# Row-centred squares: stores issued from ScalarE's queue in pairs of rows

## The chip, the cores and the metric

The kernel runs on one core of a Trainium2 chip. The metric is device time in microseconds (us) of that core. The kernel before takes 82.98 us, the median of three runs that lie between 82.96 and 83.04 us. A separate profiled execution took 83.14 us; its span, from the first to the last recorded instruction, is 81.4 us. All times of single instructions below are counted from the start of that span.

## What is computed

```python
def reference(x, axis):                       # x: 1024 x 4096, float32; axis = -1
    mean = np.mean(x, axis=axis, keepdims=True)
    return ((x - mean) ** 2).astype(np.float32)
```

Every row of 4096 numbers is averaged, the average is subtracted from the row, and the differences are squared. The input is 16.78 MB and so is the output; every byte is read once from HBM (the chip's memory) and written once.

## The kernel before

The 1024 rows are split into two tiles. A tile has 128 partitions, and each partition holds four whole rows (`Q = 4`), 4 x 4096 numbers or 64 KB. Both tiles have a buffer of their own, so that both loads can be asked for at the start, and the squares are written over the input in the same buffer.

```python
x_t = x.rearrange("(p n q) d -> n p (q d)", p=P, q=Q)
out_t = out.rearrange("(p n q) d -> n p (q d)", p=P, q=Q)

for i in range(ntiles):                       # ntiles = 2
    x_tile = io.tile([P, Q * D], F32)
    if i == 0:
        nc.sync.dma_start(out=x_tile[:, :HEAD], in_=x_t[i][:, :HEAD])       # HEAD = 512 numbers
        nc.sync.dma_start(out=x_tile[:, HEAD:], in_=x_t[i][:, HEAD:])
    else:
        end = Q * D - HEAD
        nc.scalar.dma_start(out=x_tile[:, end:], in_=x_t[i][:, end:])
        nc.sync.dma_start(out=x_tile[:, :end], in_=x_t[i][:, :end])
    # ... (tiles.append)
```

A load is thus one large transfer of 62 KB for each partition, issued from SP's queue, and a small one of 2 KB for each partition. The small one of the second tile is issued from ScalarE's queue. Then each row (128 rows at a time, one in each partition) takes two steps: VectorE (DVE in the profile) adds it up and yields minus the mean; ScalarE (ACT) squares the row with that as its bias. Of the fourth row of a tile, VectorE does the last eighth.

```python
for i in range(ntiles):
    for q in range(Q):
        row = tiles[i][:, q * D:(q + 1) * D]
        # ... (pairs, neg_mean: scratch and one number for each partition)
        inorder(nc.vector.tensor_tensor_reduce(out=pairs, in0=row[:, :HALF], in1=row[:, HALF:],
                scale=-inv_d, ..., accum_out=neg_mean))                    # L66
        cut = D if q < Q - 1 else LAST
        nc.scalar.activation(out=row[:, :cut], in_=row[:, :cut], func=ACT.Square,
                bias=neg_mean, scale=1.0)                                  # L77
        if cut < D:
            rest = row[:, cut:]
            nc.vector.tensor_scalar_add(out=rest, in0=rest, scalar1=neg_mean)   # L86
            nc.vector.tensor_mul(out=rest, in0=rest, in1=rest)                  # L87
    nc.sync.dma_start(out=out_t[i], in_=tiles[i])                          # L88: one store a tile
```

A framework places the semaphore waits and orders each engine's instructions; it may move an instruction among its neighbours on the same engine.

Of the kernel before, what the change touches and what calls it, by code (L numbers as in the profile page):

```python
# [2 lines left out]

os.environ.setdefault("NEURON_RT_ULTRASERVER_MODE", "4")

# [4 lines left out]

F32 = mybir.dt.float32
ACT = mybir.ActivationFunctionType
ADD = mybir.AluOpType.add


@with_exitstack
def kernel(
    ctx: ExitStack,
    tc: tile.TileContext,
    x: bass.AP,  # L20
    axis: bass.AP,
    out: bass.AP,
):

    nc = tc.nc

    B, D = x.shape
    P = nc.NUM_PARTITIONS
    Q = 4
    HEAD = 512
    HALF = D // 2
    LAST = D - D // 8
    assert B % (P * Q) == 0
    ntiles = B // (P * Q)
    inv_d = 1.0 / float(D)

    x_t = x.rearrange("(p n q) d -> n p (q d)", p=P, q=Q)
    out_t = out.rearrange("(p n q) d -> n p (q d)", p=P, q=Q)

    io = ctx.enter_context(tc.tile_pool(name="io", bufs=ntiles))
    scratch = ctx.enter_context(tc.tile_pool(name="scratch", bufs=1))
    stats = ctx.enter_context(tc.tile_pool(name="stats", bufs=ntiles * Q))

    tiles = []
# [3 lines that stand above are left out]
            nc.sync.dma_start(out=x_tile[:, :HEAD], in_=x_t[i][:, :HEAD])  # L52
# [5 lines that stand above are left out]
        tiles.append(x_tile)  # L58

    inorder = tc.keep_in_program_order  # L60
# [3 lines that stand above are left out]
            pairs = scratch.tile([P, HALF], F32)  # L64
            neg_mean = stats.tile([P, 1], F32)
            inorder(nc.vector.tensor_tensor_reduce(  # L66
                out=pairs,
                in0=row[:, :HALF],
                in1=row[:, HALF:],
                scale=-inv_d,  # L70
                scalar=0.0,
                op0=ADD,
                op1=ADD,
                accum_out=neg_mean,
            ))
            cut = D if q < Q - 1 else LAST
            nc.scalar.activation(  # L77
                out=row[:, :cut],
                in_=row[:, :cut],
                func=ACT.Square,  # L80
                bias=neg_mean,
                scale=1.0,
            )
            if cut < D:
                rest = row[:, cut:]
                nc.vector.tensor_scalar_add(out=rest, in0=rest, scalar1=neg_mean)  # L86
                nc.vector.tensor_mul(out=rest, in0=rest, in1=rest)  # L87
        nc.sync.dma_start(out=out_t[i], in_=tiles[i])  # L88


# [1 line left out]
_INS = ['x', 'axis']  # L92
_OUTS = [((1024, 4096), 'float32')]

_NUMBERS = {'axis': -1}


# [26 lines left out]
```

## Time and profile before

| | before |
|---|---|
| device time, median of 3 | 82.98 us |
| profiled span | 81.4 us |
| VectorE busy | 20.8 us (26%) |
| ScalarE busy | 29.4 us (36%) |
| DMA queue of SP (q1) | 33.29 MB |
| DMA queue of ScalarE (q10) | 0.26 MB |
| HBM read / written | 16.78 MB / 16.78 MB |
| bytes per time over the span | 412 GB/s |

How to read it: a core has 16 DMA engines, and both queues feed them. The profile names the two queues by number: q1 is SP's and q10 is ScalarE's. A "packet" of the DMA records is one piece that a DMA engine moves at once; here it is the part of a transfer that belongs to one partition, so a transfer over 128 partitions is 8 packets on each of the 16 engines, and a last record of 4 bytes on each engine counts the semaphore that tells of completion. An issuing instruction (L53, L57, L88) only hands over a transfer: it is short, and the transfer lands later.

### The profile page before, as it was taken

Reading aid. Unit: us, or ns where it says so; the run is one execution under the profiler, and the core shown is the slowest. Engines: PE = TensorE matmul, PEld = TensorE weight load, DVE = VectorE, ACT = ScalarE, POOL = GpSimd, SP = SyncE. Lnnn points to the kernel's source line nnn. Section 1 sums busy time; section 2 is a strip of 40 time slices with the busy share of each in tenths; the row PEclk is TensorE's granted clock in tenths of the full one; section 3 lists DMA queues with packets and bytes.
Section 4 is the critical chain, followed back from the end, with each engine's and each line's share of the span. In section 5 each row is a group of like instructions: output and inputs, shape, how many; then the busy total and the mean of one; then the engine's idle time right before and its main releaser. Section 6 shows DMA issues by size and latency. Waiting matters only on the chain.

```text
span 81.4 us, 87 instructions
## 1 busy us (share of the span) xinstructions
DVE 20.8 (26%) x20; ACT 29.4 (36%) x9; POOL 0.2 (0%) x4
## 2 busy tenths in 40 slices
DVE  0000000000059999600039999700000000000000
ACT  0000000000054999999502999999600000000000
POOL 0000000000000000000000000000000000000000
DMA  1974999999759999995799993899996599999390
GB/s 22 704 343 187 499 499 499 499 499 437 343 218 499 499 499 499 499 406 250 343 516 515 515 515 161 354 515 515 515 516 290 258 483 515 515 515 419 161 451 0
DMA packets 864, 33.55 MB, mean 412 GB/s; under 512 B 96, under 2 KB 96, under 8 KB 352
## 3 DMA queue, kind: packets, MB, share of 16 engines
q1 hardware_dynamic: 720, 33.29, 95.0%
q10 hardware_dynamic: 144, 0.26, 1.1%
HBM read 16.78 MB, written 16.78 MB: 412 GB/s over the span
## 4 chain that ended last, share of the span: by engine, by line
DMA 49%; ACT 13%; ACTq 4%; DVE 3%; SPq 1%; issue 0%
DMA x_tile<-in_x_dram 49%; ACT x_tile L77 13%; ACTq L119 4%; DVE pairs L66 3%; SPq L53 1%; SPq L52 0%; DVE neg_mean L66 0%
## 5 line engine op out<-in xcount | busy, mean ns | idle before, releaser
L77 ACT ACTIVATE x_tile<-x_tile,neg_mean 128x4096 f32<-128x4096 f32 (+1 forms) x8 | 28.2, 3590 | 5.7 <-DVE neg_mean L66 5.7
L66 DVE CUSTOM_DVE_ANT_0 pairs<-x_tile 128x2048 f32<-128x2048 f32 x8 | 18.3, 2292 | 31.6 <-DMA x_tile<-in_x_dram 31.4
L77 ACT ACT_TABLE_LOAD x1 | 1.3, 1283 | 23.2 <-DMA x_tile<-in_x_dram 23.2
L87 DVE TENSOR_TENSOR x_tile<-x_tile 128x512 f32<-128x512 f32 x2 | 1.4, 692 | 0.1
L86 DVE TENSOR_SCALAR x_tile<-x_tile,neg_mean 128x512 f32<-128x512 f32 x2 | 1.0, 488 | 0.1
L66 DVE DVE_READ_ACCUMULATOR2_ANT neg_mean<- 128x1 f32 x8 | 0.7, 82 | 0.0
L105 POOL MEMSET const-bfloat16-1.0<- 128x1 bf16 x1 | 0.1, 102 | 0.0
L105 POOL MEMSET const-uint8-127<- 128x1 uint8 x1 | 0.1, 102 | 0.0
L105 POOL MEMSET const-float32-0.0<- 128x1 f32 x1 | 0.1, 99 | 0.2 <-issue 0.2
L105 POOL MEMSET const-float32-1.0<- 128x1 f32 x1 | 0.1, 99 | 0.0
## 6 DMA issues: line engine op xcount, KB each, us to landing
x_tile<-in_x_dram SPq DMA_DIRECT2D x2, 7936.0 KB, 31.1
x_tile<-in_x_dram ACTq DMA_DIRECT2D x1, 256.0 KB, 3.8
x_tile<-in_x_dram SPq DMA_DIRECT2D x1, 256.0 KB, 3.6
out_dram<-x_tile SPq DMA_DIRECT2D x2, 21.9
```

What stands on the lines that cost most here:

```text
L53: nc.sync.dma_start(out=x_tile[:, HEAD:], in_=x_t[i][:, HEAD:])
L66: inorder(nc.vector.tensor_tensor_reduce(out=pairs, in0=row[:, :HALF], in1=row[:, HALF:], scale=-inv_d, scalar=0.0, op0=ADD, op1=ADD, accu ...
L77: nc.scalar.activation(out=row[:, :cut], in_=row[:, :cut], func=ACT.Square, bias=neg_mean, scale=1.0,)
L86: nc.vector.tensor_scalar_add(out=rest, in0=rest, scalar1=neg_mean)
L87: nc.vector.tensor_mul(out=rest, in0=rest, in1=rest)
L105: nc = _bacc.Bacc("TRN2", target_bir_lowering=False, num_devices=1)
L119: with _tile.TileContext(nc) as tc:
```

## The change

The store of a whole tile from SP's queue at the end of the tile is removed. In its place, after every second row, two rows (32 KB for each partition) are stored from ScalarE's queue. Two stores of 8.39 MB become four of 4.19 MB; the bytes are the same. The aim is that squared rows leave while the second tile is still being loaded, and that SP's queue holds loads alone, so that a store need not stand behind a load.

```diff
             if cut < D:
                 rest = row[:, cut:]
                 nc.vector.tensor_scalar_add(out=rest, in0=rest, scalar1=neg_mean)
                 nc.vector.tensor_mul(out=rest, in0=rest, in1=rest)
-        nc.sync.dma_start(out=out_t[i], in_=tiles[i])
+            if q % 2 == 1:
+                part = slice((q - 1) * D, (q + 1) * D)
+                nc.scalar.dma_start(out=out_t[i][:, part], in_=tiles[i][:, part])
```

In the built program, ScalarE's instructions then stand in this order (the rows of the first tile are r0 to r3, those of the second s0 to s3; the stores are A, B, C and D):

```
square r0, r1, r2
store A (r0, r1)      waits for the squares of r0 and r1
square r3
wait for the second tile's large load
square s0             waits for VectorE's mean of s0
store B (r2, r3)      waits for the square of r3
square s1, s2
store C (s0, s1)      waits for the squares of s0 and s1
square s3
store D (s2, s3)      waits for VectorE's part of s3 and for the square of s3
```

## The prediction, made before the changed kernel had run

> **What bounds the kernel now.** I read the engine totals first, then the chain of waits, then the queue's own waits, and last the busy times by stretch, because the first three name a suspect and only the last shows whether it is full.
>
> The page's totals show no compute engine near its limit:
>
> ```profile
> DVE 20.8 (26%) x20; ACT 29.4 (36%) x9; POOL 0.2 (0%) x4
> q1 hardware_dynamic: 720, 33.29, 95.0%
> q10 hardware_dynamic: 144, 0.26, 1.1%
> DMA 49%; ACT 13%; ACTq 4%; DVE 3%; SPq 1%; issue 0%
> ```
>
> The first line is busy time; the next two are the DMA queues with packets, MB and share of 16 engines' span, 96.1% together; the last is the chain that ended last. Its shares add up to only about 71%, or 58 us: the chain stops at the issue of the last store, at 58.4 us. What follows stands in the queue's own waits:
>
> ```profile
> SPq L88 <- DVE x_tile L87: 41.8, 2, 29.4
> SPq L119 <- DMA out_dram<-x_tile: 21.7, 2, 19.3
> SPq L88 <- ACT x_tile L77: 11.7, 2, 5.8
> ```
>
> The middle line is the end of the kernel waiting for the last store to land. The third line looks like a chance: SP waits for ScalarE before it may issue a store. But whether an earlier issue would help depends on whether the DMA engines are idle meanwhile. So I asked for stretches: from the first load's regular packets to its end, the whole second load, the first store, and all from the first packet to the last.
>
> ```profile
> core 0: us, DVE busy (x) ACT busy (x) POOL busy (x), PEclk, DMA share, GB/s
> 4.08:22.79 18.71, 0.00 (x0) 0.00 (x0) 0.00 (x0) 1.00 1.00 434
> 22.79:41.50 18.71, 10.38 (x10) 15.36 (x5) 0.00 (x0) 1.00 1.00 433
> 40.93:60.25 19.32, 10.38 (x10) 14.08 (x4) 0.00 (x0) 1.00 1.01 434
> 1.74:80.25 78.51, 20.76 (x20) 29.44 (x9) 0.00 (x0) 1.00 1.00 427
> 80.25:81.40 1.15, 0.00 (x0) 0.00 (x0) 0.00 (x0) 1.00 0.00 0
> ```
>
> The last two columns before the line's end are the share of the 16 DMA engines that is busy, and GB/s. They are full, share 1.00, from 1.74 to 80.25 us, through loads and stores alike. Where the first store follows the second load, at 40.93 to 41.50 us, no engine has a gap: SP had issued that store at 39.73 us, before the load was out. The dips in the page's 40 slices, down to 161 GB/s, are only the beat of long packets: a packet is counted in the slice where it starts, and a 62 KB packet takes 2.34 us. **The bound is the sum of bytes through 16 full DMA engines**, with 1.74 us ahead and 1.15 us after.
>
> **What the Trainium skill says.** "DMA: Bandwidth & Descriptors", section "Issuing engines are not separate DMA queues": transfers issued by different engines run on the same 16 DMA engines, and a second issuing engine saves only issue time. The trace agrees as far as it goes: an issue lasts 0.35 to 0.42 us, in the shade of a transfer. The same page, "Where 436 GB/s comes from", puts the ceiling at 435.2 GB/s; the trace has 434 for loads and for stores. The same page, "Queues, rings and completion order": each engine takes packets from its queues in turn. The trace agrees at the start, where 2 KB packets of q1 and q10 alternate on an engine, one by one and 84 ns long mostly, so with no visible cost of changing queues; there both were loads. "Perfetto Trace Analysis", section "DMA Instruction — HWDGE (DVE, Sync)": a DMA engine here doesn't wait on semaphores, the issuing sequencer does. So waits on ScalarE's queue hold back the stores behind them. No run so far shows that for a store on ScalarE's queue.
>
> **The change, part by part.** (1) *Packet cost.* Per packet the trace has 84 ns for 2,048 bytes, 2,342 ns for 63,488 and 2,418 ns for 65,536. A straight line through the first two has 36.75 ps a byte and 8.7 ns fixed, and gives 2,417 ns for the third, so it holds. A new store packet of 32,768 bytes then takes 1,213 ns, two of them 2,426 against 2,418. Each engine has 16 store packets now and 32 after: 16 more at 8.7 ns is 0.14 us; two more completion records of 9 ns make it 0.16 us. No byte is saved.
>
> (2) *Store A.* ScalarE squares r0 and r1 from 25.63 us; two squares take 7.31 us (the chain's own piece for the second tile), so the issue is at 32.9 us instead of 39.73. The first load took 1.0 us from its issue at 0.73 to its first packet at 1.75, so A's packets come at about 34.0. The second load's packets start at 22.2 us and every 2.34 us after; the sixth of eight starts at 33.9, so about three of A's packets get between the load's last three. The load lands 3 x 1.21 = 3.6 us later, at 45.1 instead of 41.5, and the squares of the second tile start at 44.25 + 3.64 = 47.9. This loses nothing by itself: DMA engines do other bytes in that time.
>
> (3) *Store B.* It is ready when r3 is squared, 39.7 us, but stands behind ScalarE's wait for the second load and behind the square of s0. It is issued between 45.6 us (load landed, plus the 0.42 us that VectorE took to start) and 47.9 us, with packets 1.0 us later, 48.9 at worst. At 45.1 us five of A's packets are left, 5 x 1.21 = 6.1 us, enough until 51.2 us (50.6 on the earliest engines). So B is there 1.7 us before the engines would run dry.
>
> (4) *Stores C and D.* Squares of s0 and s1 end at 47.9 + 7.3 = 55.2 us, and C is wanted when B's eight packets are through, 51.2 + 9.7 = 60.9. All squares end at 47.9 + 14.1 = 62.0, and D is wanted at 70.6. Both have slack, so ScalarE's four issues (0.35 us each) and the 3.6 us later start are off the path. D's packets then end at 80.3 to 80.4 us, against 80.25 before.
>
> *Sum.* 82.98 + 0.16 for packets + about 0.1 for changes of direction, below: 83.2 us. The intended gain has no place to come from, because the first store never waited behind idle DMA engines.
>
> **The rivals.** *A. Engines run dry before B.* Turn-taking by packet is seen for equal packets only. If instead the two queues share by bytes, the load's last 7.5 us become 15.0, it lands at 49.0, A has 2.2 us left, and B's packets come at up to 49.4 + 2.3 (one row sum of 2.29) + 1.0 = 52.7, which is 1.5 us late: 84.7 us. If stores had the right of way, the load would land at 51.2 and B come at 54.9: 3.7 us, or 86.9. The order of instructions speaks for this rival, the alternating packets at the start against it; and if ScalarE's sequencer goes past the square of s0 to issue B while that square waits, 2.3 us of it vanish.
>
> *B. Loads and stores together are faster than either alone.* They go in opposite directions, and 434 GB/s was seen with one direction at a time. If reads and writes didn't share a limit, the load's 7.5 us would be hidden beside A: as low as 75 to 76 us. Against it: loads and stores run at the same 27.1 GB/s for an engine, as one limit inside the engine would make it, and at the crossing at 41 us nothing went faster.
>
> *C. Mixing directions costs.* At that crossing 11 of the 16 first store packets took 2,453 to 2,465 ns instead of 2,418, 40 ns more. With some six changes of direction on an engine this is up to 0.24 us; I took 0.1 of it. If every packet of the stretch is slowed by several per cent, it is half a microsecond.
>
> *D. ScalarE becomes the bound.* It would need D's issue later than 70 us; 8.6 us of slack speak against it.
>
> **Range and chances.** The low end, 82.8, allows the 0.16 us to be hidden and some noise; the high end, 84.7, is B late by sharing in bytes. Within 2% is 81.3 to 84.6, which holds my account with and without rival C. Slower by over 2% needs most of rival A: 0.10. Faster by over 2% needs rival B: 0.04. The rest is 0.86.
>
> **What would show it.** In the changed profile: DMA share still 1.00 in every stretch from 1.7 to 80 us, at 434 GB/s; q10 with about 17 MB; store packets of 1.21 us; the second load landing near 45 us and the first row sum of the second tile starting near 45.6; B issued between 45.6 and 47.9; the last landing near 80.4 and a span of 81.6. A share below 1 near 50 us is rival A, and shows how late B came; over 450 GB/s between 34 and 45 us is rival B; packets above 1.25 us there are rival C. I'd be wrong above all if packets of unlike size aren't taken in turn, or if opposite directions don't share the engine's limit.

## The result, and the profile after

The changed kernel takes 84.92 us, median of six runs (84.81 to 85.32), beside 82.98 us for the kernel before (82.93 to 83.04). The ratio is 1.0245, with a 95% interval of 1.0219 to 1.0271: slower by 1.94 us. The prediction was 83.2 us with a range of 82.8 to 84.7, and 0.86 for "within 2%"; the measured time lies above the range.

The page of the changed kernel, the same parts as before (busy time, queues, chain):

```profile
DVE 20.8 (25%) x20; ACT 29.4 (35%) x9; POOL 0.2 (0%) x4
q1 hardware_dynamic: 432, 16.52, 48.6%
q10 hardware_dynamic: 720, 17.04, 47.7%
DMA 55%; DVE 10%; issue 6%; ACT 4%; SPq 1%; ACTq 0%
```

The compute engines do the same work in the same time, and the stores' 16.78 MB have moved from q1 to q10, as they should. The chain now has 55% of waiting for loads where it had 49%. The timeline of the changed kernel around the second tile (start, duration, engine, line, instruction, and in brackets what ended the idle time before it) shows what became of the load and of store B:

```profile
32.87 0.34 ACTq L90 DMA_DIRECT2D out_dram<-x_tile  x1
...
47.16 2.29 DVE L66 CUSTOM_DVE_ANT_0 pairs<-x_tile 128x2048 f32<-128x2048 f32 x1 [13.42 <-DMA x_tile<-in_x_dram]
...
49.50 3.71 ACT L77 ACTIVATE x_tile<-x_tile,neg_mean 128x4096 f32<-128x4096 f32 x1 [9.89 <-DVE neg_mean L66]
49.50 0.34 ACTq L90 DMA_DIRECT2D out_dram<-x_tile  x1
...
56.83 0.34 ACTq L90 DMA_DIRECT2D out_dram<-x_tile  x1
...
63.60 0.34 ACTq L90 DMA_DIRECT2D out_dram<-x_tile  x1
```

Store A is issued at 32.87 us, as computed. The second tile's first row sum starts at 47.16 us, not 45.6. Store B is issued at 49.50, in the very instant in which the square of s0 starts: it did stand behind that square's wait. The obvious suspicion, that the DMA engines ran dry before B, is answered by the stretches of the changed kernel (columns as in the prediction; a packet is counted where it starts):

```profile
33.70:41.56 7.86, 0.04 (x1) 5.91 (x2) 0.00 (x0) 1.00 0.98 325
42.80:81.00 38.20, 10.37 (x10) 14.08 (x4) 0.00 (x0) 1.00 1.00 434
```

The second stretch, which has B's start in it, is full at 434 GB/s. In the first one the engines are as full, share 0.98, but move 325 GB/s. **Busy and slow together: the packets themselves took longer.** The packet records say which. From 5 us to the end of the stores no engine is idle for more than 0.01 us. The 16 load packets that began at 33.8 to 34.5 us took 2.82 to 3.80 us instead of 2.34, the next 16 took 2.54 to 3.81; the last 16, from 41.56 us on, took 2.34 again, although they took turns with store packets, and every store packet took 1.213 us. All load packets together lasted 31.3 us longer than in the kernel before, which is 1.96 us on each of the 16 engines; 1.83 of it lies in the first 32 of those packets, the rest in excesses of under 0.2 us elsewhere.

That accounts for the loss. Load packets +1.96 and store packets +0.03 make 1.99 us for an engine. The last store packet ended at 81.89 us instead of 80.23, 1.66 later, and the large load packets of this profile began 0.34 us earlier than in that of before (3.13 instead of 3.47). What remained was why load packets were stretched, once, when the stores joined.

### The profile page after: what moved, and what is told of

The parts are those of the page before. It is cut to its first block, busy times and chain, and to the rows that moved or that the text cites. A ratio compares the mean times of both kernels' runs of the same rounds, so it can differ in the third digit from the quotient of the medians.

```text
span 83.0 us, 88 instructions
## 1 busy us (share of the span) xinstructions
DVE 20.8 (25%) x20; ACT 29.4 (35%) x9; POOL 0.2 (0%) x4
## 3 DMA queue, kind: packets, MB, share of 16 engines
HBM read 16.78 MB, written 16.78 MB: 404 GB/s over the span
## 4 chain that ended last, share of the span: by engine, by line
DMA 55%; DVE 10%; issue 6%; ACT 4%; SPq 1%; ACTq 0%
DMA x_tile<-in_x_dram 55%; DVE pairs L66 8%; ACT x_tile L77 4%; DVE x_tile L87 1%; DVE x_tile L86 1%; SPq L53 1%; SPq L52 0%; DVE neg_mean L66 0%; ACTq L90 0%
```

## The experiments

Theories at the start: **mixing** (a load packet is slow for as long as stores run beside it), **start-up** (the joining of stores costs once), **compute** (ScalarE's squaring in the same buffers slows a two-way transfer), **queue** (sharing engines between two queues costs). The first runs added **early queueing** (stores cost if they wait on an engine that still has load packets to begin) against **packet size**. "Stretch" below is what load packets, or store packets where named, lasted over 2.342 us (62 KB), 1.213 (32 KB) or 2.418 (64 KB), summed and divided by 16 engines; up to 0.23 us of it lies in small excesses of single packets away from the joining. The ratios are to the kernel before as it ran beside each group: 82.98 us for the changed kernel, 83.10 to 83.12 us for the others. Kernels called copies leave all computing out and store the input itself; their profile lines have no columns for VectorE and ScalarE.

| kernel | time, us | ratio to before | load stretch, us |
|---|---|---|---|
| before | 82.98 | 1 | 0.00 |
| changed | 84.92 | 1.022 to 1.027 | 1.96 |
| pairs_sp | 84.55 | 1.016 to 1.019 | 1.51 |
| late_pairs_sp | 83.34 | 1.002 to 1.004 | 0.01 |
| whole_act | 83.71 | 1.004 to 1.009 | 0.09 |
| late_pairs_act | 83.84 | 1.006 to 1.010 | 0.00 |
| copy_act | 84.41 | 1.015 to 1.018 | 1.35 |
| copy_sp | 84.64 | 1.017 to 1.023 | 1.48 |
| copy_whole_sp | 84.40 | 1.015 to 1.018 | 1.54 |
| copy_whole_act | 84.42 | 1.015 to 1.020 | 1.34 |
| copy_two_loads | 84.83 | 1.019 to 1.023 | 0.00 |

**1. Pairs, from SP's queue.**

```diff
-                nc.scalar.dma_start(out=out_t[i][:, part], in_=tiles[i][:, part])
+                nc.sync.dma_start(out=out_t[i][:, part], in_=tiles[i][:, part])
```

> The four stores of two rows, but issued from SP's queue, so that each stands behind the second load and never beside it. In the changed kernel the load packets that met store packets on the same DMA engine took up to 3.8 us instead of 2.34, and all 256 large load packets together took 31.4 us more, which is 1.96 us on each of 16 engines: the whole loss. If meeting is the cause (theory: mixing), this kernel has every load packet at 2.34 us and the time of before plus 16 packets x 8.7 ns, 83.1 us. If smaller stores are the cause, 84.9 us.

Measured: 84.55 us, and stretched load packets although no store packet had begun. Stores didn't pass the load on this queue: A was issued at 32.87 us and stood behind the load's last packets. Those last 16 took 3.40 to 3.93 us and no other took over 2.52; the earliest of them was over, 1.2 us late, when the first store packet began at 42.27 us. The stretch from the first of them to that store packet:

```profile
38.60:42.26 3.66, 0.00 (x0) 1.01 (x1) 0.00 (x0) 1.00 0.99 278
```

Full again, and slow: 278 GB/s, with loads alone moving. So the mixing theory falls as I had stated it, and so does the change of queue as the whole cause: without it, 1.43 us are lost (84.55 against 83.12).

**2. Copies: stores early, without computing.** In place of the loop over rows:

```diff
+    for i in range(ntiles):
+        for h in range(2):
+            part = slice(2 * h * D, 2 * (h + 1) * D)
+            nc.scalar.dma_start(out=out_t[i][:, part], in_=tiles[i][:, part])
```

copy_sp has `nc.sync` there.

> Nothing is computed: the two loads as they are, and the four stores from ScalarE's queue as soon as the tile has landed, so A and B start near 24 us and meet all eight of the second load's packets on each engine. Theory mixing: load packets are stretched by about 1 us each for as long as stores run beside them, seven or eight packets, 7 us in all, so 88 to 91 us. Theory start-up (the first store on a queue that joins costs once): 2 us, so 85 us, with two stretched packets on an engine and the rest at 2.34. Theory compute (ScalarE's squaring in the same buffers slows the transfers when they go both ways): no packet is stretched, 83 us.

> Nothing is computed; the same four stores from SP's queue, where A and B stand behind the second load. All theories: 83.0 to 83.2 us, load packets 2.34 us; it is the base for the copies and shows that the squaring isn't in the sum.

Measured: 84.41 and 84.64 us. ScalarE and VectorE do nothing in either, so the compute theory falls. In copy_act, A and B were issued from 23.2 us; the stretches at their joining and after:

```profile
24.40:27.74 3.34, 0.00 (x0) 1.00 1.00 304
32.06:49.50 17.44, 0.00 (x0) 1.00 0.98 427
```

304 GB/s while the stores join, then 427 GB/s for 17 us in which loads and stores take turns on every engine, packet by packet. Turn-taking in opposite directions was free here; the joining cost, once, 1.35 us. In copy_sp my expectation of 83 us was wrong like that of pairs_sp: the last load packets, next to the waiting stores, took 3.43 to 4.03 us.

**3. Two loads on two queues.**

```diff
-            nc.sync.dma_start(out=x_tile[:, :end], in_=x_t[i][:, :end])
+            nc.scalar.dma_start(out=x_tile[:, :end], in_=x_t[i][:, :end])
```

(as a copy, stores from SP's queue)

> Nothing is computed; the second tile's large load is issued from ScalarE's queue at the start, so that two loads share the engines from the first microsecond, and the stores come after from SP's queue. If sharing an engine between two queues costs whatever the direction, load packets here are stretched and the time is 85 us or more. If it is the meeting of loads with stores (mixing), packets stay at 2.34 us and the time at 83 us, plus up to 1 us if the stores' issue comes after both loads have landed.

Measured: 84.83 us, but for another reason: all load packets kept 2.34 us on both queues, and the engines stood idle for 1.7 us each between 41 and 43 us, because the stores could only be issued (41.92 us) when both loads had landed; the store packets were another 0.24 us too long in sum. Two queues in one direction cost the load packets nothing, and this is how a true gap looks: idle engines, not long packets.

**4. Late issue, and whole tiles early.** late_pairs_sp cuts the stores of the kernel before, without issuing them earlier; whole_act changes its queue alone; the two copies store whole tiles early.

```diff
-        nc.sync.dma_start(out=out_t[i], in_=tiles[i])
+        for h in (1, 0):                                  # late_pairs_sp
+            part = slice(2 * h * D, 2 * (h + 1) * D)
+            nc.sync.dma_start(out=out_t[i][:, part], in_=tiles[i][:, part])
```

```diff
-        nc.sync.dma_start(out=out_t[i], in_=tiles[i])
+        inorder(nc.scalar.dma_start(out=out_t[i], in_=tiles[i]))   # whole_act; the squares in order too
```

> The kernel before with each tile's store cut into two stores of two rows, still at the end of the tile from SP's queue, rows 2 and 3 first, so that none is issued before 39.7 us. Every kernel so far whose stores were queued on the DMA engines while several load packets were outstanding lost 1.3 to 2.0 us once, in the load packet or two ahead of the first store packet; the kernel before, issuing at 39.73 us, lost none, but its packets are 64 KB. Theory early queueing: this kernel issues late, so its load packets keep 2.34 us and it takes 83.1 us (0.16 us for packets). Theory packet size (32 KB packets start badly): 84.5 us, load packets up to 3.5 us.

> The kernel before with its whole-tile stores issued from ScalarE's queue, each right behind the square of the tile's last row (at 39.7 us, as before): the change of queue alone. The store's first 64 KB packets then take turns with the second load's last packet or two. Theory early queueing: two load packets at most are outstanding, so little is lost, 83.0 to 83.6 us. Theory packet size: 83.0 us. Theory that ScalarE's queue itself costs: 84.5 us or more.

> Nothing is computed; whole-tile stores, 64 KB packets, from SP's queue, the first asked for near 23 us, behind the whole second load. Theory early queueing: the load packet ahead of the first store packet is stretched to 3.5 us as in the copy with 32 KB packets, 84.4 us. Theory packet size: no load packet above 2.4 us, 83.0 us.

> Nothing is computed; whole-tile stores, 64 KB packets, from ScalarE's queue, the first asked for near 23 us, taking turns with the second load from then on. Theory early queueing: one or two load packets on each engine stretched, then clean turns, 84.4 us. Theory packet size: 83.0 us.

Measured: 83.34 and 83.71 us with late issue; 84.40 and 84.42 with 64 KB packets asked for early, load packets stretched by 1.54 and 1.34 us much as with 32 KB. Packet size falls, early queueing stands. The issues, first of pairs_sp and then of late_pairs_sp (all four stores are merged into one line):

```profile
32.87 27.22 SPq L90 DMA_DIRECT2D out_dram<-x_tile  x4
```

```profile
39.69 20.20 SPq L90 DMA_DIRECT2D out_dram<-x_tile  x4
```

Against the line of pairs_sp above, the same place in late_pairs_sp, the last load packets up to the first store packet:

```profile
38.50:40.94 2.44, 0.00 (x0) 1.16 (x1) 0.00 (x0) 1.00 0.90 390
```

This is the regular beat: packets of 62 KB that take 2.34 us each. The line counts only 15 of the last 16, because one began at 38.49 us, so its share is under 1 and its GB/s are not to be set against the 278 as they stand. The last load packet began at 39.09 us, so no load packet was left to begin when the stores came. The two kernels differ in when the first tile's stores were issued, 32.87 against 39.69 us, and in the order of the two. From ScalarE's queue a late store has a smaller price, paid in its own first packets: in whole_act the first 16 took 2.46 to 3.47 us, and store packets were stretched by 0.50 us in sum (0.09 in the kernel before).

**5. The changed kernel, issued late.**

```diff
+        for h in (1, 0):                        # after the four squares of the tile, kept in order
+            part = slice(2 * h * D, 2 * (h + 1) * D)
+            inorder(nc.scalar.dma_start(out=out_t[i][:, part], in_=tiles[i][:, part]))
```

> The changed kernel with its early issue alone taken away: four stores of two rows from ScalarE's queue, but both stores of a tile only after the square of its last row (39.6 us for the first tile), ahead of the wait for the second load. Theory early queueing: the stores join when no load packet but the last is left on an engine, so 83.3 to 83.7 us, between the pairs issued late from SP's queue (83.34) and the whole tiles issued late from ScalarE's (83.71). If ScalarE's queue and pairs of rows together cost, 84.9 us.

Measured: 83.84 us, ratio 1.0083 (1.0064 to 1.0103). The kernel before took 83.10 us beside it, so with pairs and ScalarE's queue kept and the early issue taken away, 1.2 of the 1.94 us come back. No load packet is stretched; the remaining 0.74 us is mostly first store packets (store packets were stretched by 0.53 us in sum, up to 2.31 us for a packet of 1.213, in an execution of 84.13 us, the longest of four).

The four kernels that store in pairs make a table of two by two. Each number is the loss in us against the kernel before as it ran beside them:

| | issued late | issued early |
|---|---|---|
| SP's queue | 0.24 | 1.43 |
| ScalarE's queue | 0.74 | 1.94 |

Early issue costs 1.2 us on either queue, and ScalarE's queue 0.5 us at either time. So early issue is the larger part of the loss and not all of it. The order of the two stores changes together with the time of issue here; but the whole tiles of copy_whole_sp, which have no such order, were stretched when issued early and not in the kernel before. The copies don't show the price of the queue (84.41 us from ScalarE's, 84.64 from SP's); why it is paid in the full kernel is open.

**6. How often, how long, and for small packets.** copy_tiny_act puts a store of 2 KB packets ahead near 4 us; copy_small_loads cuts the second load into row-sized ones; copy_fifo4 has four tiles and passes from load to store three times.

```diff
+    nc.scalar.dma_start(out=out_t[0][:, :HEAD], in_=tiles[0][:, :HEAD])        # copy_tiny_act
```

```diff
+            for a in range(0, end, D):                                         # copy_small_loads
+                e = min(a + D, end)
+                nc.sync.dma_start(out=x_tile[:, a:e], in_=x_t[i][:, a:e])
```

```diff
-    Q = 4
+    Q = 2
...
+        if i > 0:                                                              # copy_fifo4
+            nc.sync.dma_start(out=out_t[i - 1], in_=tiles[i - 1])
```

> The copy with stores from ScalarE's queue near 23 us, but ahead of them one small store (the first 512 numbers of each partition's first row, 2 KB packets, landed first) that is asked for near 4 us, while the first load runs. Theory first store ever: what is lost is lost once at 4 us, by packets of the first load, and the join at 24 us is clean (no load packet there above 2.4 us). Theory each join: load packets near 25 us are again stretched by some 1.3 us in sum on each engine, as without the small store.

> The same copy with the second tile's large load cut into four of one row each, so load packets of 16 KB (about 0.61 us) instead of 62 KB. If what is lost when the stores join is a fixed time on each engine, the time stays at 84.4 us (plus 0.2 for packets), spread over several packets. If it is the packet or two that stand next to the first store packet, of whatever size, the loss shrinks to a quarter, 83.4 to 83.7 us.

> Nothing is computed; four tiles of two rows, and all transfers on SP's queue in the order load 0, load 1, store 0, load 2, store 1, load 3, store 2, store 3, each store asked for as soon as its tile has landed, so that it stands behind a load that still has most of its packets. The engines pass from load to store three times and back twice. Theory once (only the first joining of stores costs): 84.4 to 84.8 us, one layer of stretched load packets. Theory each passage from load to store: three such layers, 87 us or more.

Measured: copy_fifo4 84.91 us (84.63 to 85.79). The issue of the store of its second passage from load to store, and then the first and the second passage:

```profile
23.93 0.34 SPq L58 DMA_DIRECT2D out_dram<-x_tile  x1
```

```profile
18.80:22.90 4.10, 0.00 (x0) 1.00 0.96 264
38.90:43.90 5.00, 0.00 (x0) 1.00 1.00 426
```

The first is slow (packets stretched by 1.42 us in sum), the second at the usual rate (0.07 us), though the store stood there early as well, and at the third no packet is long: in this kernel the cost came once. copy_small_loads took 86.19 us: load packets near 25 us were stretched by 1.4 us in sum although each is about a quarter as long, so the loss is a time and not a number of packets; a further 1.5 us is a true gap between 71 and 74 us, because the turns with small load packets had let both stores run out (at 56.2 us) long before the load had landed. copy_tiny_act took 84.28 us (83.67 to 84.45): the small store took its turns from 4 to 23 us without disturbing any load packet, so a first store of 2 KB packets doesn't pay the price ahead. The large store's joining then stretched load packets by 0.8 us. That is the execution of 83.67 us; the other three took 84.21 to 84.45, about as long as copy_act (84.41), so it isn't shown that a small store ahead lessens the loss.

**7. Which side of a store does it.** Three kernels, each profiled in a single execution, in which one transfer of 4.19 MB joins the second load behind a store of 16 small packets; the remaining stores follow when both loads have landed.

```diff
+    inorder(nc.scalar.dma_start(out=out_t[0][:16, last], in_=tiles[0][:16, last]))
+    inorder(nc.scalar.dma_start(out=out_t[0][:, :2 * D], in_=tiles[0][:, :2 * D]))   # join_store
+    inorder(nc.scalar.dma_start(out=out_t[0][:, :2 * D], in_=x_t[0][:, :2 * D]))     # join_dram instead
+    inorder(nc.scalar.dma_start(out=spare, in_=tiles[0][:, :2 * D]))                 # join_sbuf instead
```

> Nothing is computed. Near 23.5 us one transfer of 4.19 MB joins the second load from ScalarE's queue, behind a store of 16 small packets that only holds it back until the first load has landed; the other stores follow from SP's queue when both loads have landed. Here the joining transfer is a store (SBUF to HBM), the control: load packets near 25 us should be stretched by 1.0 to 1.5 us in sum on each engine. The end of the kernel isn't what is read.

> The same, but the joining transfer copies the same rows from the input to the output within HBM: it writes HBM and doesn't read SBUF. If writing HBM is what disturbs the loads, load packets are stretched as in the control; if reading SBUF is, they keep 2.34 us at the join.

> The same, but the joining transfer copies the same rows from one SBUF buffer to another (4.19 MB more moved in all): it reads SBUF and doesn't write HBM. If reading SBUF is what disturbs the loads, load packets are stretched as in the control; if writing HBM is, they keep 2.34 us; if both keep or both stretch, the side isn't told.

Measured: in all three the first large joining packets began near 32 us. The load packets just ahead of them, first of join_store and then of join_dram:

```profile
29.20:32.60 3.40, 0.00 (x0) 1.00 1.00 300
```

```profile
29.20:31.63 2.43, 0.00 (x0) 1.00 0.97 419
```

And join_sbuf, where some packets of the joining transfer fall into the stretch as well:

```profile
31.75:35.60 3.85, 0.00 (x0) 1.00 1.08 332
```

Load packets were stretched by 1.09 us in join_store, 0.11 in join_dram (next to none of it at the joining, most of it near 40 us) and 1.94 in join_sbuf (up to 3.85 us for a packet). So in these executions writing HBM was not enough to disturb the loads at the joining, and the two transfers that read SBUF did disturb them, whatever they wrote. Whether it is SBUF as such, or that the joining transfer reads another memory than the loads do, isn't told apart. The times, 84.68, 83.54 and 95.07 us (join_sbuf moves 4.19 MB more), aren't needed for that.

## Why the prediction was wrong, point by point

*What bounds the kernel, and that no gain was to be had*: right. The DMA engines are full in both kernels, and loads beside stores moved 427 GB/s in copy_act, not more than either alone (rival B falls).

*(1) Packet cost*: right in size. A 32 KB packet took 1.213 us, as computed.

*(2) Store A, "this loses nothing by itself"*: this is **the step that failed**. The issue came as computed, but A's first packets began at 37.2 us, not 34.0: on every engine the load packet that began at 33.8 to 34.5 us went first, and it took up to 3.8 us instead of 2.34. In the sum it is the term "about 0.1 for changes of direction", rival C, that was mis-sized: 1.96 us were measured where I had put 0.1 and thought half a microsecond the worst. The sign I had named for it, store packets above 1.25 us, didn't come either: every store packet took 1.213 us, and it was the loads that were stretched. The experiments put 1.2 us of the loss on the early issue and 0.5 on ScalarE's queue. I had taken its size from the crossing of the kernel before, the 40 ns on first store packets, without seeing that there the store had been issued (39.73 us) when the last load packets were already moving. That crossing couldn't show what a store costs that waits while load packets are still to begin, and the early issue is what the change adds.

*The load's landing*: expected at 45.1, used at 47.16. The last load packets ended at 45.58 us, near the forecast, but by luck: only two of A's packets, not three, had got between the load's last three, which is 1.2 us less, and the stretch added 1.96. Then the load's completion record, in its turn, stood behind one store packet: the last record is at 46.80 us. I had left that 1.2 us out; it cost nothing at the end, since C and D were still issued in time.

*(3) Store B*: right that it isn't late. It was held until s0's square started, 49.50 us, 1.6 us after the latest time I had named, but A ran later too: A's completion records came at 52.38 to 52.85 us and B's packets followed without a gap. Rival A, the one for which I had given most of my chance of "slower", didn't happen.

*(4) C, D and rival D*: right; the last issue was at 63.60 us and its packets weren't due before 71.7.

*What is open*: the runs show that a stream of large packets that reads SBUF, put on engines that have HBM loads to begin, holds up those loads by 0.8 to 2.0 us once, and that late issue avoids it (0.00 to 0.09 us of load stretch). How it does so is open: in pairs_sp the load packets were held up before any store packet had begun, and no run shows what the engines do in that time. Why it isn't paid again at a second passage, and how many load packets must still be to begin, is open too: no kernel issued its first store between 33 and 39 us.

## What to carry to other kernels

When every DMA engine is full from first byte to last, there is no idle time for earlier stores to fill; here the early issue only decided what they met. Look for packet durations, not only for gaps: a stretch with a busy share of 1 and fewer GB/s than its neighbours has long packets in it. And take the price of a new overlap from a place where that same overlap already happens; a crossing that happens late doesn't price an early one.

## What the runs showed of the hardware that I had not expected

- A store issued early stretched load packets even where it could only stand behind them in the same queue: 3.40 to 3.93 us instead of 2.34 (pairs_sp).
- Turn-taking between loads and stores on two queues was one packet for one packet at every size tried (62 KB against 64, 32 and 2 KB, 16 KB against 32), and was free once it ran: 427 GB/s over 17 us in copy_act. So 2 KB packets behind 62 KB ones wait long: the small store of copy_tiny_act, issued at 3.95 us, had its last packet at 23.2 us.
- A store's issue on ScalarE's queue didn't pass a square that waited: 49.50 us for both, 2.3 us after the load was there.
